# A hybrid decoder layer on one core: an ordering model with a shared port, fewer two-input operations on Pool, and 1/RMS spread by transposes

## The chip, the core and the metric

The kernel runs on 1 core of one Trainium2 chip. The metric is the device time of one execution in microseconds (us). In the profile the engines are PE (TensorE, matrix products; PEld its weight loads), DVE (VectorE), ACT (ScalarE), POOL (GpSimd) and SP (SyncE, which here only starts DMAs). Each engine works through its own queue in order and waits at an instruction until what that instruction needs is there.

## What is computed

One layer of a decoder for a prompt of 1024 tokens and 8 sample sequences of 8 tokens, with shared weights, all in float32. The tokens stand together as 1088 columns.

```python
hn = _rmsnorm(x, lw['norm1_g'])
z = hn @ lw['w_in']                      # q | k | v | u_ssm | u_pool
...                                      # dilated attention, merged over three dilations
...                                      # S5 state space: complex diagonal scan, GELU, GLU
...                                      # trailing mean pooling, linear map
mix = jnp.concatenate([_rmsnorm(att, lw['out_norm_att']),
                       _rmsnorm(ssm_out, lw['out_norm_ssm']),
                       _rmsnorm(pool_out, lw['out_norm_pool'])], axis=-1)
x = x + mix @ lw['w_out']
hn2 = _rmsnorm(x, lw['norm2_g'])
up = hn2 @ lw['w_up']
up_c, conv_state = _causal_dwconv(up, conv_prefix, lw['conv_w'], lw['conv_b'])
a, g = jnp.split(up_c, 2, axis=-1)
x = x + (jax.nn.silu(g) * a) @ lw['w_down']
```

The model width is 1024, the feed-forward width 2816. A last RMSNorm follows, and the new K, V, state, pooling and convolution buffers are outputs too.

## The kernel before

**Products.** Features lie on the 128 partitions, tokens on the free axis. A float32 product is done as three products of operands in two parts: the high part is a cast by ACT, the low part the difference (a two-operand subtraction by DVE or Pool). The split weights of a half tile are called `whl` (three buffers), those of the activations `A`. The input projection, the output projection and the first tiles of the up projection go by `dense_group`: 24 products into one PSUM bank `dps` (two banks), token chunk by token chunk (384, 384 and 320 columns). The rest of the up projection and the down projection are taken in 2 x 2 blocks by seven products (`wino`, Winograd's form), in PSUM banks `wX`, `wY`, `wW`. This needs sums of blocks: of the tokens' features once (`tgen`, tiles X, then `tsplit` into T and A), of the up weights (`uraw`, `wraw`), of the down weights (`draw`, `wraw`, in `dsum` and `dw`) and of the hidden features (`hst`, staged back from memory four tiles at a time, in `hb`), the last two followed by splits into `whl` and `hop`. Each of the 20 steps of the down projection has 14 outputs, which DVE adds to `X` straight from PSUM.

**Beside the products** run, as generators, the parts of the layer that are no large products: the SSM (`ssm_params` and `ssm_tables`: tables of powers, many small operations on Pool; table products `s_pn` on DVE; transposes `rps`; then the scan, the products `yps`, a round trip through memory, GELU, and the products `glu`), prompt attention (scores `S`, transposes `tp`, products `pv`), sample attention, pooling, and the norms. A norm sums squares on PE (`nps`), computes 1/RMS (`rs_x`, `rs_t`, `rs_y`) and spreads it over all partitions on PE (`bcast`, into `nbc`).

**What sets the order.** The program is put down by a planner of its own. `Model.note` (line 87) is called for each instruction before it is issued, from `call` (line 154), and estimates from a table of costs when the instruction will start and end: its engine's queue, when its operands are ready, and a delay between engines. All instructions but DMA starts therefore carry line 156 in the profile, and one goes by the tiles' names. `Driver` steps the generators: each yields the time at which its next step can run, and `tick`, called between products, steps those whose time has come by the model's clock of PE; `until` steps others while a product cannot go on. Which engine makes a two-operand step is chosen by `light(d)` (line 1607): Pool if by the model it would be free `d` us earlier than DVE. `d` is -0.5 for the features' sums and splits, 0 for the down weights' sums, -0.5 and 0.5 for the hidden features' sums and splits, 0.5 for the down weights' splits, 2.5 for the gate, 9 for the up weights. The order on each engine is fixed when the program is built; on the chip only semaphores act.

Of the kernel before, what the change touches and what calls it, by code (L numbers as in the profile page):

```python
# [12 lines left out]
P = 128  # L13
# [22 lines left out]
class Model:  # L36
    """Estimates when each instruction will run; the order in which the independent parts of the kernel
    are put down goes by it."""
    LAT = 0.13
    OWN = {"pe": 0.0, "dve": 0.1}  # L40

    def __init__(self):
        self.free = {}
        self.mem = {}
        self.ring = {}
        self.dma = 0.0
        self.tiled = False

# [9 lines left out]
    def ready(self, *aps, eng=None):  # L58
        """When the last writes to aps are done, as seen by an engine."""
        t = 0.0  # L60
        for ap in aps:
            m, lo, hi = self.seg(ap)
            for b in range(lo, hi + 1):
                if b in m[1]:
                    f, e = m[1][b]
                    t = max(t, f + self.LAT if e != eng else f + self.OWN.get(e, 0.1) if e != "dma" else 0.0)
        return t
# [18 lines left out]

    def note(self, eng, fn, args, kw):
# [14 lines left out]
        else:  # L102
            if eng == "pe":
# [4 lines left out]
                elif args[1].dtype == F32R:  # L108
                    c = 0.0034 + n / 2400.0
                else:  # L110
                    c = 0.005 + max(4 * n / 2400.0, 0.213 * max(np_, 32) / 128.0)
                if np_ < P:
                    # column tiles run beside the first
# [19 lines left out]
            else:  # L133
                c = 0.15 + (2.0e-3 if fn == "tensor_tensor" else 3.35e-3) * n
# [50 lines left out]
class Driver:  # L185
    """Steps the generators of the parts that run beside the large products.  A generator yields when
    its next step can run: a time, a condition, or None for at once."""
# [24 lines left out]
    def pick(self, t):  # L212
        """The generator to step: by priority among those ready at t, else the next to be ready."""
# [26 lines left out]
class Body:  # L240
# [8 lines left out]
    def acq(self, n):  # L249
        """Waits for n PSUM banks of the common ring."""  # L250
# [6 lines left out]
    def act(self, c, q, k):  # L257
        """The high (q = 0) or low part of feature tile k of the activations, token chunk c."""
# [9 lines left out]
    def rsqrt(self, x, n, width, pool=False):  # L268
        """x: [n, width] SBUF, overwritten; gives 1/sqrt(x).  pool: on Pool, else on DVE."""
# [26 lines left out]
    def rstd(self, c, parts, segs, pool=False):  # L296
        """1 / RMS of token chunk c: parts(k0, k1, a) gives the squares to be summed for segment
        (k0, k1, scale), as APs of [128, 128 tokens from a]."""
# [20 lines left out]
    def bcast(self, c, y, bc=None):  # L319
        """y [tokens of a tile, tile] of chunk c as [128, tokens], the same on every partition."""  # L320
# [3 lines left out]
        for ti, (a, w) in enumerate(self.tok_tiles(c)):  # L324
            last = CH[c][1] == 320 and ti == 2
            nc.tensor.matmul(bc[:, a + (64 if last else 0):a + 128], y[:, ti:ti + 1].to_broadcast([P, 128]),
                             self.ident[:, 64:128] if last else self.ident[:, :], start=True, stop=True)
        return bc

# [1 line left out]
    def w_open(self, src, n, alloc=None):  # L331
        """src(i): DRAM AP [128, 4, 128] of half tile i; n: number of halves."""
# [40 lines left out]
    def w_split(self, upto):  # L373
        """Starts the splits of the product's halves before upto."""
# [6 lines left out]
    def dense_group(self, m, c, out_fn, last=True, pool=None):  # L381
        """One (feature tile, token chunk) of a product with K = 1024; last: the tile's last chunk."""
# [5 lines left out]
        for k in range(KD):  # L388
# [11 lines left out]
            if k == 3 and last:  # L400
                if self.w_hold < self.ws["n"]:
                    # the first of the two tiles that share the chunks
# [9 lines left out]
    def prep(self, c, src, gcol):  # L412
        """The activations of chunk c times the gains, in two parts; the RMS is divided out after the
        product."""
# [10 lines left out]
    def put_rms(self, c, y, own=False):  # L425
        """1 / RMS of chunk c to its place, the same on every partition."""
# [10 lines left out]
    # ---------------------------------------------------------------- SSM parameters  # L437
    def pfma(self, out, x, a, y, t):
        """out = x * a + y on Pool (a: immediate)."""
# [4 lines left out]
    def horner(self, p, cs, r):  # L444
        """p = (..((p + c0) * r + c1) * r ..) * r on Pool."""
# [21 lines left out]
    def cmul(self, eng, orr, oi, ar, ai, br, bi, t):  # L467
        """(orr, oi) = (ar + i ai) * (br + i bi); orr, oi differ from the operands; t: scratch."""
# [7 lines left out]
    def ssm_params(self):  # L476
# [48 lines left out]
        # powers of the decay, 0..8  # L525
# [21 lines left out]
        # decay^8 of the modulus, rotation^(8 * 2^k)  # L547
# [10 lines left out]
        # input matrix  # L558
# [20 lines left out]
        # C of both groups of a pair, each with zeros on the other one's states  # L579
# [7 lines left out]
    def ssm_tables(self, hf):  # L587
        """Tables of one half (4 pairs of groups)."""
# [18 lines left out]
        yield None  # L607
        ar, ai = bt(self.pwp[:, 0, q, :]), bt(self.pwp[:, 1, q, :])
        cr, ci = bch(self.bc_in[:, 2, q, :]), bch(self.cneg[:, q, :])
        # the real and the negated imaginary part of C a^n; cneg holds the negated imaginary part of C  # L610
# [11 lines left out]
        # R with (step, channel) on the partitions  # L622
# [10 lines left out]
        # impulse response blocks  # L633
# [38 lines left out]
    def ssm_half(self, hf):  # L672
# [30 lines left out]
        # sample sequences: one chunk each  # L703
# [19 lines left out]
        # rotate back; column c of the chunk buffer holds the state before chunk c  # L723
# [76 lines left out]
    # ---------------------------------------------------------------- pooling mixer  # L800
    def pool_open(self):
        """The scratch is the K and V memory of the next pair."""
# [20 lines left out]
    def pool_in(self, i, c, ps):  # L823
        """Takes chunk c of the pooling input to its buffer, behind the 15 columns before it."""
# [61 lines left out]
    # ---------------------------------------------------------------- prompt attention  # L886
    def att_scores(self, j):
        """Scores of the query blocks and their exponentials; the products with V follow in att_out.
# [1219 lines left out]
def _layout(a):  # L2108
# [6 lines left out]
    out = {}  # L2115
# [94 lines left out]
```

## Time and profile before

| | us |
|---|---|
| time, median of 3 runs (lowest to highest) | 1363.84 (1362.06 to 1365.27) |
| span of the profiled execution | 1362.6 |
| PE busy | 1272.4 |
| DVE busy | 1031.8 |
| POOL busy | 566.7 |
| ACT busy | 539.4 |

The span of the profiled execution, from the first to the last instruction, lies inside the range of the runs' times. By time the stages are: 0 to 80 the norm of the input, the first projections and the SSM's small tables; 80 to 250 input projection beside SSM and prompt attention; 250 to 570 the rest of it, sample attention, the output projection and the second norm; 570 to 640 the first tiles of the up projection and the block sums of its operands; 640 to 1040 the up projection in blocks; 1040 to 1320 the down projection in blocks; then the last pair of tiles and the final norm.

### The profile page before, as it was taken

Reading aid. Unit: us, or ns where it says so; the run is one execution under the profiler, and the core shown is the slowest. Engines: PE = TensorE matmul, PEld = TensorE weight load, DVE = VectorE, ACT = ScalarE, POOL = GpSimd, SP = SyncE. Lnnn points to the kernel's source line nnn. Section 1 sums busy time; section 2 is a strip of 40 time slices with the busy share of each in tenths; the row PEclk is TensorE's granted clock in tenths of the full one; section 3 lists DMA queues with packets and bytes.
Section 4 is the critical chain, followed back from the end, with each engine's and each line's share of the span. In section 5 each row is a group of like instructions: output and inputs, shape, how many; then the busy total and the mean of one; then the engine's idle time right before and its main releaser. Section 6 shows DMA issues by size and latency. Waiting matters only on the chain.

```text
span 1362.6 us, 26926 instructions
## 1 busy us (share of the span) xinstructions
PE 1272.4 (93%) x10466; PEld 1182.9 (87%) x10466; DVE 1031.8 (76%) x1990; ACT 539.4 (40%) x1127; POOL 566.7 (42%) x914
## 2 busy tenths in 40 slices
PE   7699899999999899978999999999999788888997
PEld 7697787777767899977999999999999688888997
DVE  5536765564378932897888888898889989999866
ACT  6222333333245422443545445455454333333333
POOL 7860430210012422593233232332335978768624
PEclk9899999999999999988999999999999889999997
DMA  9221212578874345202231221212212513222213
GB/s 339 87 81 33 68 40 83 183 240 289 281 246 149 83 138 157 65 24 102 106 112 55 88 82 62 95 65 79 95 49 99 186 56 113 97 68 91 81 44 132
DMA packets 80319, 154.84 MB, mean 114 GB/s; under 512 B 9856, under 2 KB 43136, under 8 KB 80192
## 3 DMA queue, kind: packets, MB, share of 16 engines
q1 hardware_dynamic: 78960, 149.68, 33.1%
q10 hardware_dynamic: 1152, 3.04, 0.6%
q8 instruction: 82, 1.34, 0.4%
q14 instruction: 45, 0.37, 0.1%
q0 software_dynamic: 80, 0.41, 0.1%
HBM read 124.04 MB, written 28.47 MB: 112 GB/s over the span
## 4 chain that ended last, share of the span: by engine, by line
PE 68%; DVE 18%; POOL 7%; issue 4%; DMA 1%; ACT 1%; POOLq 0%; DVEq 0%; SPq 0%; ACTq 0%
PE wX L156 23%; PE dps L156 15%; PE wY L156 11%; PE wW L156 5%; DVE X L156 5%; DVE whl L156 3%; POOL ssm_small L156 3%; DVE hop L156 2%; PE pv L156 2%; PE dn L156 2%; PE S L156 2%; DVE P L156 1%; PE yps L156 1%; PE od L156 1%; PE Sp L156 1%
## 5 line engine op out<-in xcount | busy, mean ns | idle before, releaser
L156 PE MATMUL dps<-A,whl 128*128 128x384 f32 (+1 forms) x1896 | 370.3, 344 | 29.7 <-DVE k L156 11.9
L156 PEld LDWEIGHTS dps<-A,whl 128*128 128x128 f32 x1896 | 319.9, 194 | 51.0 <-issue 14.9
L156 PE MATMUL wX<-T,whl 128*128 128x272 f32 x1440 | 193.0, 290 | 4.8 <-DVE whl L156 3.7
L156 PEld LDWEIGHTS wX<-T,whl 128*128 128x128 f32 x1440 | 186.1, 190 | 5.6 <-DVE whl L156 4.1
L156 PE MATMUL wX<-hop,whl 128*128 128x272 f32 x960 | 141.8, 300 | 27.1 <-DVE X L156 21.8
L156 PEld LDWEIGHTS wX<-hop,whl 128*128 128x128 f32 x960 | 130.8, 196 | 32.8 <-issue 12.1
L156 DVE SCALAR_TENSOR_TENSOR cv<-raw,vec,cv 128x1104 f32<-128x1104 f32 x88 | 126.0, 1431 | 12.2 <-ACT cv L156 10.8
L156 POOL TENSOR_TENSOR th<-th,cv 128x64 f32<-128x64 f32 (+1 forms) x40 | 79.8, 2013 | 131.2 <-DVE th L156 127.4
L156 PE MATMUL wY<-A,whl 128*128 128x272 f32 x960 | 127.6, 288 | 0.9 <-DVE whl L156 0.9
L156 PEld LDWEIGHTS wY<-A,whl 128*128 128x128 f32 x960 | 123.3, 188 | 1.1 <-DVE whl L156 1.1
L156 ACT CAST whl<-uraw 128x512 fp32r<-128x512 f32 x120 | 74.8, 623 | 81.0 <-PE wX L156 44.2
L156 ACT CAST whl<-draw 128x256 fp32r<-128x256 f32 (+1 forms) x122 | 47.8, 415 | 143.4 <-POOL draw L156 33.3
L156 POOL COPY cvo<-raw 128x2 f32<-128x2 f32 x88 | 27.6, 343 | 167.2 <-DVE raw L156 154.9
L156 ACT CAST whl<-wraw 128x512 fp32r<-128x512 f32 (+1 forms) x92 | 52.3, 570 | 112.4 <-PE dps L156 63.7
L156 DVE TENSOR_TENSOR whl<-uraw,whl 128x512 fp32r<-128x512 f32 x120 | 87.2, 727 | 12.5 <-ACT whl L156 9.9
L156 DVE TENSOR_TENSOR whl<-wraw,whl 128x512 fp32r<-128x512 f32 (+1 forms) x90 | 67.0, 745 | 31.2 <-ACT whl L156 31.2
L156 DVE TENSOR_TENSOR X<-wX,X 128x272 f32<-128x272 f32 x160 | 66.6, 431 | 14.3 <-PE wX L156 14.0
L156 PE MATMUL wY<-hop,whl 128*128 128x272 f32 x480 | 69.1, 293 | 1.0 <-DVE whl L156 1.0
L156 DVE TENSOR_TENSOR uraw<-uraw 128x512 f32<-128x512 f32 x40 | 69.2, 1729 | 0.7
L156 PEld LDWEIGHTS wY<-hop,whl 128*128 128x128 f32 x480 | 64.6, 193 | 1.6 <-DVE whl L156 1.6
L156 ACT ACTIVATE P<-P,sm 128x128 f32<-128x128 f32 (+7 forms) x64 | 35.7, 558 | 74.0 <-DVE sm L156 74.0
L156 PE MATMUL wW<-A,whl 128*128 128x272 f32 x480 | 63.2, 288 | 0.0
(271 smaller groups left out, 2336.1 us busy)
## 6 DMA issues: line engine op xcount, KB each, us to landing
K<-in_ck_dram SPq DMA_DIRECT2D x40, 512.0 KB, 6.3
V<-in_cv_dram SPq DMA_DIRECT2D x80, 256.0 KB, 4.4
uraw<-in_w_up_dram SPq DMA_DIRECT2D x40, 512.0 KB, 4.0
hs<-th SPq DMA_DIRECT2D x22, 544.0 KB, 2.7
hst<-hs SPq DMA_DIRECT2D x22, 544.0 KB, 5.3
draw<-in_w_down_dram SPq DMA_DIRECT2D x20, 512.0 KB, 3.5
wraw<-in_w_in_dram SPq DMA_DIRECT2D x28, 256.0 KB, 3.1
X<-xs SPq DMA_DIRECT2D x8, 544.0 KB, 4.4
```

The costliest lines, as they stand in the source:

```text
L156: return f(*args, **kw)
```

## The change

**The model's costs.** PE's products of split operands are taken as 0.447 ns for each column (0.417 before), other float32 products a little longer, Pool's two-operand operations as 2.2 ns for each column (2.0 before), and the delay of a result to the same engine as 0.12 us on DVE and Pool (0.1 before).

**The port.** The model now keeps the intervals in which DVE and Pool use a port that they share. Of DVE these are the operations without an operand in PSUM (`two`), of Pool all but memsets. An operation that would start inside an interval of the other engine is taken to start at its end (`clear`).

**Pool's share.** `light(d)` takes Pool only where it would be free more than 2 us before DVE, and never for `d` of 9.

**SSM tables.** The step that makes the products with `ssm_pwp` and `ssm_cneg` on DVE is due when the model has these two ready; before, it was due at once.

**The broadcast of 1/RMS** is three transposes of the column of values, repeated over the columns, in place of three float32 products of it with the identity.

Comments and docstrings are taken out too, which shifts line numbers: line 156 of before is line 174 of after.

```diff
 class Model:
-    OWN = {"pe": 0.0, "dve": 0.1}
+    OWN = {"pe": 0.0, "dve": 0.12, "pool": 0.12}
...
+        self.port = {"dve": [], "pool": []}
+
+    def clear(self, eng, t):
+        other = self.port["pool" if eng == "dve" else "dve"]
+        for a, b in reversed(other[-40:]):
+            if a <= t < b:
+                return self.clear(eng, b)
+        return t
...
+    def two(self, args, kw):
+        x = [a for a in list(args[1:]) + [kw.get("in0"), kw.get("in1")] if hasattr(a, "bitcast") and a.free_size() > 1]
+        return all(a.space != bass.MemoryType.PSUM for a in x)
...
                 elif args[1].dtype == F32R:
-                    c = 0.0034 + n / 2400.0
+                    c = 0.0034 + 0.447e-3 * n
                 else:
-                    c = 0.005 + max(4 * n / 2400.0, 0.213 * max(np_, 32) / 128.0)
+                    c = 0.005 + max(4 * n / 2350.0, 0.218 * max(np_, 32) / 128.0)
...
             else:
-                c = 0.15 + (2.0e-3 if fn == "tensor_tensor" else 3.35e-3) * n
+                c = 0.15 + (2.2e-3 if fn == "tensor_tensor" else 3.35e-3) * n
+            if eng == "pool" and fn != "memset" or eng == "dve" and self.two(args, kw):
+                start = self.clear(eng, start)
+                self.port[eng].append((start, start + c))
...
     def bcast(self, c, y, bc=None):
         for ti, (a, w) in enumerate(self.tok_tiles(c)):
-            last = CH[c][1] == 320 and ti == 2
-            nc.tensor.matmul(bc[:, a + (64 if last else 0):a + 128], y[:, ti:ti + 1].to_broadcast([P, 128]),
-                             self.ident[:, 64:128] if last else self.ident[:, :], start=True, stop=True)
+            nc.tensor.transpose(bc[:, a:a + 128], y[:, ti:ti + 1].to_broadcast([P, 128]), self.ident)
...
     def ssm_tables(self, hf):
         self.cmul(g, rn[:, 0], rn[:, 1], ar, ai, br, bi, t4)
-        yield None
+        yield self.M.ready(self.pwp, self.cneg)
...
     def light(self, d=0.0):
-        return self.nc.gpsimd if self.M.free.get("pool", 0.0) + d < self.M.free.get("dve", 0.0) else self.nc.vector
+        return self.nc.gpsimd if max(d, 2.0) < 9.0 and self.M.free.get("pool", 0.0) + 2.0 < self.M.free.get("dve", 0.0) else self.nc.vector
```

**What moves.** Counted over the whole program, 81 two-operand operations go from Pool to DVE: 48 with 256 columns in the down projection (`draw`, `wraw` and their splits), 18 sums of `hst` and 4 splits `hop` there, ten of the block sums and splits of the up projection's operands (`X`, `T`, `A`), and one of the final norm (`acc`). Besides, a few evictions of PSUM change between DVE and ACT. PE has the same products; the order of the small ones among the dense ones shifts.

The first place is DVE's queue about 50 us in, at the SSM's first tables (`s_pn`, and X_92 as scratch); `k_671` is the K tile that evicts the dense products `dps`. Before:

```order
L156 SCALAR_TENSOR_TENSOR X_85<-dps,rms 128x64
L156 TENSOR_TENSOR s_pn<-ssm_pwp,bc_in 128x512
L156 TENSOR_TENSOR X_92<-ssm_pwp,ssm_cneg 128x512
L156 TENSOR_TENSOR s_pn<-s_pn,X_92 128x512
L156 TENSOR_TENSOR s_pn<-ssm_pwp,ssm_cneg 128x512
L156 TENSOR_TENSOR X_92<-ssm_pwp,bc_in 128x512
L156 TENSOR_TENSOR s_pn<-s_pn,X_92 128x512
L156 TENSOR_TENSOR whl<-wraw,whl 128x512
L156 TENSOR_TENSOR k_671<-dps,rms 128x384 x2
L156 TENSOR_TENSOR whl<-wraw,whl 128x512
L156 TENSOR_TENSOR k_671<-dps,rms 128x320
```

and after:

```order
L174 SCALAR_TENSOR_TENSOR X_85<-dps,rms 128x64
L174 TENSOR_TENSOR whl<-wraw,whl 128x512
L174 TENSOR_TENSOR k_671<-dps,rms 128x384 x2
L174 TENSOR_TENSOR s_pn<-ssm_pwp,bc_in 128x512
L174 TENSOR_TENSOR X_92<-ssm_pwp,ssm_cneg 128x512
L174 TENSOR_TENSOR s_pn<-s_pn,X_92 128x512
L174 TENSOR_TENSOR s_pn<-ssm_pwp,ssm_cneg 128x512
L174 TENSOR_TENSOR X_92<-ssm_pwp,bc_in 128x512
L174 TENSOR_TENSOR s_pn<-s_pn,X_92 128x512
L174 TENSOR_TENSOR whl<-wraw,whl 128x512
L174 TENSOR_TENSOR k_671<-dps,rms 128x320
```

One weight split and the first two evictions of K, which stood behind the six table products, stand ahead of them; the third eviction stays behind. On PE the transposes `rps` that follow come after 39 dense products counted from the end of the second K chunk, and after 42 before.

The second place is PE's queue ahead of the first `glu` of the SSM, about 235 us in. Before, after the last `yps`:

```order
L156 MATMUL vps<-ident,vT 128x128 x3
L156 MATMUL dps<-A_74,whl 128x320 x2
L156 MATMUL dps<-A_82,whl 128x320
L156 MATMUL vps<-ident,vT 128x128 x4
L156 MATMUL pv<-P,v_674 64x128 x4
L156 MATMUL pv<-P,vf_676 64x32 x8
L156 MATMUL S<-k_672,X_86 128x256 x2
L156 MATMUL S<-k_672,X_86 32x192 x8
L156 MATMUL dps<-A_75,whl 128x320 x2
L156 MATMUL dps<-A_83,whl 128x320
L156 MATMUL glu<-X_91,s_t 128x408
L156 MATMUL glu<-X_92,s_t 128x408
```

and after (the last dense product ahead of `glu` stands eight rows ahead of the first one shown):

```order
L174 MATMUL tp<-ident,P 32x128
L174 MATMUL tp<-ident,P 128x128 x2
L174 MATMUL S<-k_672,X_86 128x256 x2
L174 MATMUL S<-k_672,X_86 32x192 x8
L174 MATMUL pv<-P,v_674 64x128 x4
L174 MATMUL pv<-P,vf_676 64x32 x16
L174 MATMUL tp<-ident,P 128x128
L174 MATMUL tp<-ident,P 64x128
L174 MATMUL tp<-ident,P 128x128 x3
L174 MATMUL tp<-ident,P 64x128
L174 MATMUL tp<-ident,P 128x128 x2
L174 MATMUL glu<-X_91,s_t 128x408
```

The dense products between the last `yps` and the first `glu` fall from 54 to 21, and what stands right before `glu` is attention alone. The last `yps` come 36 dense products later than before, and the second half's transposes `rps` 24 later.

The third place is Pool's queue in the down projection, where the second group of hidden features comes in (`hst` their sums, `hop` their split, `draw` and `whl` the weights' sums and splits). Before:

```order
L156 TENSOR_TENSOR draw<-draw 128x256
L156 TENSOR_TENSOR whl<-draw,whl 128x256 x3
L156 TENSOR_TENSOR draw<-wraw,draw 128x256
L156 TENSOR_TENSOR hop<-hst,hop 128x544
L156 TENSOR_TENSOR hst<-hst 128x544 x5
L156 TENSOR_TENSOR whl<-draw,whl 128x256
L156 TENSOR_TENSOR hst<-hst 128x544
L156 TENSOR_TENSOR draw<-wraw,draw 128x256
L156 TENSOR_TENSOR hop<-hst,hop 128x544 x2
```

and after:

```order
L174 TENSOR_TENSOR whl<-draw,whl 128x256 x2
L174 TENSOR_TENSOR hop<-hst,hop 128x544
L174 TENSOR_TENSOR hst<-hst 128x544 x3
L174 TENSOR_TENSOR whl<-draw,whl 128x256
L174 TENSOR_TENSOR hst<-hst 128x544
L174 TENSOR_TENSOR hop<-hst,hop 128x544 x2
L174 TENSOR_TENSOR whl<-draw,whl 128x256
L174 TENSOR_TENSOR hst<-hst 128x544
L174 TENSOR_TENSOR hop<-hst,hop 128x544
```

The sums of `hst` came five in a row and one more; now three, one and one, with fewer of the weights' operations between. The rest of these sums stand on DVE.

## Rows read from the trace of the kernel before

**Rows 1.** The page's first part: busy us (share of the span), instructions.

```profile
PE 1272.4 (93%) x10466; PEld 1182.9 (87%) x10466; DVE 1031.8 (76%) x1990; ACT 539.4 (40%) x1127; POOL 566.7 (42%) x914
```

**Rows 2.** Busy us by stage (start:end, length), then PEclk, DMA share, GB/s.

```profile
0.00:80.00 80.00, 60.16 (x338) 58.70 (x338) 41.21 (x102) 32.01 (x59) 61.63 (x222) 0.91 0.58 199
80.00:250.00 170.00, 163.95 (x1476) 136.86 (x1476) 105.07 (x262) 53.35 (x132) 42.84 (x112) 0.97 0.20 56
250.00:570.00 320.00, 310.59 (x3124) 258.99 (x3123) 190.40 (x556) 108.19 (x254) 71.58 (x135) 1.00 0.59 191
570.00:640.00 70.00, 55.36 (x314) 53.59 (x313) 63.23 (x66) 31.42 (x60) 47.65 (x51) 0.89 0.18 60
640.00:1040.00 400.00, 400.00 (x3185) 400.00 (x3185) 350.01 (x473) 196.66 (x362) 118.81 (x188) 1.00 0.24 82
1040.00:1290.00 250.00, 219.38 (x1595) 212.17 (x1594) 233.91 (x411) 93.18 (x210) 197.57 (x178) 0.95 0.29 99
1290.00:1362.00 72.00, 62.91 (x446) 62.57 (x444) 47.95 (x125) 24.61 (x52) 26.61 (x31) 0.90 0.25 89
```

**Rows 3.** What PE waited for: us in total, times, longest.

```profile
PE wX L156 <- DVE X L156: 21.8, 15, 4.0
...
PE dps L156 <- DVE whl L156: 11.3, 4, 7.1
```

**Rows 4.** Timeline, 1102 to 1112: start, us, engine, operation [idle before <-releaser].

```profile
1102.32 8.07 POOL L156 TENSOR_TENSOR hst<-hst 128x544 f32<-128x544 f32 x5
...
1102.93 3.33 DVE L156 TENSOR_TENSOR hop<-hst,hop 128x544 fp32r<-128x544 f32 x2
...
1106.53 2.67 DVE L156 TENSOR_TENSOR whl<-draw,whl 128x256 fp32r<-128x256 f32 x2
...
1110.04 2.38 PE L156 MATMUL wX<-hop,whl 128*128 128x272 f32 x9 [4.03 <-DVE X L156]
...
1110.85 0.41 DVE L156 TENSOR_TENSOR whl<-draw,whl 128x256 fp32r<-128x256 f32 x1
```

**Rows 5.** Groups by form, 1040 to 1160: count, busy us, mean ns, idle before.

```profile
L156 DVE TENSOR_TENSOR hst<-hst 128x544 f32<-128x544 f32 x1 | 0.7, 707 | 0.0
...
L156 POOL TENSOR_TENSOR whl<-draw,whl 128x256 fp32r<-128x256 f32 x22 | 19.1, 875 | 10.7 <-ACT whl L156 10.7
```

**Rows 6.** Timeline, 36 to 80: the stop at the SSM tables.

```profile
47.42 9.57 PE L156 MATMUL dps<-A,whl 128*128 128x320 f32 x54
...
62.85 0.55 POOL L156 TENSOR_SCALAR ssm_cneg<-bc_in 128x128 f32<-128x128 f32 x1
...
63.43 0.69 DVE L156 TENSOR_TENSOR X<-ssm_pwp,ssm_cneg 128x512 f32<-128x512 f32 x1 [12.50 <-POOL ssm_cneg L156]
...
66.88 1.54 DVE L156 TENSOR_TENSOR whl<-wraw,whl 128x512 fp32r<-128x512 f32 x1
...
68.94 9.60 PE L156 MATMUL dps<-A,whl 128*128 128x320 f32 x42 [11.95 <-DVE k L156]
...
72.80 1.28 POOL L156 TENSOR_TENSOR X<-X,X 128x512 f32<-128x512 f32 x1
```

**Rows 7.** Chain that ended last: start, us, what; one broadcast, one row of transposes.

```profile
78.54 0.87 PE rps L156 x8
...
258.63 0.79 PE nbc L156 x6
```

**Rows 8.** Timeline, 160 to 240: the second half of the SSM.

```profile
162.26 1.09 PE L156 MATMUL tp<-ident,P 128*128 128x128 f32 x8 [2.01 <-DVE P L156]
...
212.44 0.73 PE L156 MATMUL yps<-X,s_pn 64*128 64x136 f32 x4
...
231.46 1.28 DVE L156 SCALAR_TENSOR_TENSOR X<-s_rm,s_tmp 128x1088 f32<-128x1088 f32 x1
```

## The prediction

> **What bounds the kernel now.** I read the page's first part, then a table of the busy time by stage, then the list of what TensorE (PE) waited for, and then the timeline at the places that list points to. [rows 1] say that PE is the engine to look at: 1272.4 us busy of 1362.6, so at most 90 us can come from its idle time. [rows 2] say where. From 640 to 1040 PE is busy for all 400 us at the full clock: whatever else moves there, nothing can be gained. From 80 to 570 it is idle for 15 us of 490. The idle time sits in three places: 20 us before 80, 15 us from 570 to 640, 31 us from 1040 to 1290, and the granted clock falls below 1 in the same stages (0.91, 0.89, 0.95; the clock has two levels, 1.2 and 2.4 GHz, so a mean of 0.95 is a tenth of the stretch at the lower one). [rows 3] name the releaser in the last two: VectorE (DVE), by its additions into X and by its part of the weight splits. So the stages outside 640 to 1040 hang on DVE, which is 94% busy from 1040 to 1290, and the question is what the change does to DVE's queue there.
>
> **How long things take alone and beside Pool.** [rows 4] show the burst that costs most. Pool runs five sums of hst in 8.07 us, 1.61 each. In that time DVE needs 3.33 us for two operations of the size that takes 0.71 alone ([rows 5]), and 2.67 us for two of the size that takes 0.41 alone. So DVE lost 3.33 - 1.42 = 1.9 and 2.67 - 0.82 = 1.85 us, together 3.8 us beside 8.07 us of Pool, 0.47 us for each us; the additions into X stood behind it, and PE stood still for 4.03 us.
>
> **Down projection (1040 to 1290): fewer operations on Pool.** By the counts of the program 48 operations of 256 columns and 22 of 544 leave Pool for DVE here. DVE gets 48 x 0.41 + 22 x 0.71 = 35.3 us. Pool loses 48 x 0.875 ([rows 5]) + 22 x 1.61 = 77.4 of 197.6 us. At the burst's rate that gives DVE back 0.47 x 77.4 = 36.4 us, so DVE's total hardly moves (-1 us). What does change is the shape of the queue: the five sums in a row become three, one and one, and an addition into X waits behind operations of 0.4 and 0.7 us rather than behind 3.3 us. I take 3 of the 31 idle us for that. The bounds: if nothing came back, DVE would have 35 us more where it has 250 - 233.9 = 16 free, and the stage would be 19 us longer; if Pool's time all came back, the idle 31 us could go. I take a value near zero because the burst's rate, the row nearest to it, gives zero.
>
> **570 to 640: the same edit.** Ten operations, nine of 544 columns, leave Pool for DVE: about 10 x 0.71 = 7.1 us more, 0.47 x 16.1 = 7.6 us less. The weight splits that PE waits for here (11.3 us over the run, [rows 3]) stand about as far back as before, one of them behind seven sums in place of two. I take -1, from -6 to +5.
>
> **The new wait in the SSM tables.** [rows 6] show the largest single stop of PE: DVE stands at its second table product until Pool has written ssm_cneg (63.43, idle 12.50 before it), three evictions of k are queued behind it, and PE, out of PSUM banks at 57.0, is idle for 11.95 us. The change puts one weight split and two of these evictions ahead of the table products. It does not follow that 12 us are gained. PE then does the third part of k (24 products; 54 took 9.57 us, so 4.3 us, to 61.2) and half of the first part of v (12 products, 2.1 us, to 63.3). The other half of v's weights is split behind the six table products, which still begin at 63.43 and took until 66.9, and the split until 68.4. And 39 products after the stop (42 before the change) PE comes to the transposes rps, which need Pool's last table sum, done at 72.80 + 1.28 = 74.08. Before they started at 78.54; now not before 74.1. That is at most 4.4 us, and as PE is idle before them for nearly as long as before (two stops of 5 us), some of it goes to the lower clock. I take -2.5, from -4.5 to 0. What hides the rest is Pool's own chain of small operations, which the change does not touch.
>
> **1/RMS by transposes.** A broadcast of one chunk is six matrix passes of 0.79 us now; eight transposes of the same size take 0.87, so three take 0.33 ([rows 7]). That is 0.46 us less, 18 times. The first three lie before 74.1, where Pool sets the end: nothing. Nine for the mixer and three for the second norm lie where PE is 97% busy (250 to 570, [rows 2]): 12 x 0.46 = 5.5, of which I take 5.0, since the last three also wait for DVE. Of the final three the last is on the path to the end: 0.5. Together -5.5, from -2 to -8.
> On this the Trainium skill speaks against the change (TensorE: Matmul & The Clock Gate, Part 4: PE-mode transpose): it says that the full clock does not engage for a transpose as it does for a matmul. By that a broadcast would run at the lower level, 0.66 us rather than 0.33, and the twelve in the middle would gain 1.6 us rather than 5.5. Here the trace does not bear it out: by the program's order 250 to 570 holds some 180 of the 272 transposes of attention scores, at a granted clock of 1.00 ([rows 2]).
>
> **80 to 250: other order, same work.** The numbers of the planner also move SSM work against the dense products. The second half's transposes come 24 products later, which spares PE waits like the 2.01 us of [rows 8] (3.6 us in all there, with the clock at 0.97 over 170 us, 5 us). But its last yps come 36 products later, while glu must still follow the same chain: 212.4 for the last yps, 232.7 (231.46 + 1.28) for its last step on DVE ([rows 8]), 20 us. Between the two PE now has 21 dense products where it had 54, and attention, about 15 us by the durations before. So about 5 us of new idle time against 4 to 8 saved. I take 0, from -8 to +6.
>
> **The sum.** -3 - 1 - 2.5 - 5.5 + 0 = -12. The profiled execution's span, 1362.6, lies inside the runs' times, so the sum is set against the median: 1363.8 - 12 = 1352 us.
>
> **The rivals.**
> *DVE's jams dissolve.* If half of PE's 21.8 us behind the additions ([rows 3]) went, and half of what the clock costs in that stage (0.05 x 250 = 12.5), 17 us rather than 3 would be gained there: 1338. For it: DVE has idle time between the jams. Against it: DVE is 94% busy. Chance 0.12.
> *Given back.* Pool's table chain and the clock leave nothing of the first stop, glu costs 4 us, and the down projection 2 more: 1363.8 - 5.5 - 1 + 6 = 1363. This is also what one would see if the new numbers of the planner are no nearer to the chip than the old ones. Chance 0.13.
> *DVE overfull, the slower side.* With fewer Pool operations left, each meets a DVE that is more often at an operation with two SBUF operands, so what comes back for each us taken from Pool may be less than 0.47. At 0.2 DVE gets 35.3 - 15.5 = 20 us more in a stage in which it is 94% busy; the stage grows by as much, and the rest gives 9: 1375. It decides below about 0.30, where 35.3 - 0.30 x 77.4 = 12 us eat the other gains. For it: the two-operand work of DVE grows by half. Against it: the one jam that the timeline shows in full. Chance 0.16.
> *Transposes cool the clock.* Two stretches more at the lower level, 5 us each as the one from 80 to 250, where little but transposes runs, and most of the gain is gone: 1362. Against it: the clock of 1.00 from 250 to 570. Chance 0.03. This is what the rule of the Trainium skill above (TensorE: Matmul & The Clock Gate, Part 4: PE-mode transpose) would come to.
>
> **How the numbers follow.** The forecast has 0.56, its own range is 1341 to 1360. A measurement of this kernel can tell about 0.2% from no change, 2.7 us: faster is below 1361.1, slower above 1366.6. Faster: 0.56 + 0.12 = 0.68. Same: 0.13 + 0.03 = 0.16. Slower: 0.16. The range reaches from 1336, which holds nearly all of the first rival, to 1367, which holds the second and leaves out the slower one: about 0.18 outside.
>
> **What would show it.** Right: the stop before rps shorter by about 4 us and still ended by Pool; the broadcasts at 0.33 us; DVE's busy time from 1040 to 1290 within 10 us of 234 while Pool's falls from 198 to about 120; PE's waits for DVE's additions somewhat under 21.8; 640 to 1040 unchanged. Wrong: rps starting well before 74 us, DVE's busy time falling in the down projection (much more comes back than 0.47) or PE's waits for it growing (less does), or a new stop of more than 6 us ahead of glu.

## The result, and the profile after

The changed kernel takes 1376.9 us (median of 4 runs, 1373.84 to 1383.38) against 1364.55 for the kernel before, a ratio of 1.0108 with a 95% interval of 1.0085 to 1.0131: slower, where faster was forecast. The profiled execution has a span of 1372.0 us, the low end of its runs, 9.4 us over the profile of before.

The page's first part after the change answers [rows 1]; the second line is the span with the mean granted clock, which was 0.970 before.

```profile
PE 1278.6 (93%) x10412; PEld 1184.1 (86%) x10412; DVE 1041.2 (76%) x2071; ACT 538.3 (39%) x1129; POOL 466.5 (34%) x831
```
```profile
core 0: 1372.0 us, clock 0.962
```

Pool gave up 100 us, DVE took on 9. PE's idle time went from 1362.6 - 1272.4 = 90.2 to 1372.0 - 1278.6 = 93.4 us, by 3.2 only. Its busy time rose by 6.2 us, although 54 passes fewer are made. The clock explains that: (1 - clock) x span is the time at full speed that was not granted, (1 - 0.970) x 1362.6 = 40.9 us before and (1 - 0.962) x 1372.0 = 52.1 after, 11 us more (a part of it in idle time, where it costs nothing). I call it the missing clock below.

To see where, the next views cut both executions at the same places of the program: the end of `glu`, the end of the pooling map, the first block product, the first down product, the first of the last pair of tiles. Columns as in [rows 2]; before first, then after.

```profile
0.00:249.80 249.80, 223.91 (x1811) 195.36 (x1812) 146.28 (x363) 85.22 (x190) 104.48 (x334) 0.95 0.32 102
249.80:464.90 215.10, 209.75 (x2505) 159.70 (x2505) 138.92 (x445) 77.73 (x191) 36.52 (x84) 1.00 0.70 229
464.90:634.40 169.50, 153.71 (x922) 150.60 (x920) 109.12 (x170) 60.73 (x121) 80.93 (x97) 0.96 0.28 87
...
1058.00:1315.80 257.80, 229.72 (x1683) 223.16 (x1682) 234.82 (x433) 93.07 (x211) 192.25 (x179) 0.95 0.27 94
```
```profile
0.00:249.30 249.30, 222.24 (x1802) 192.88 (x1803) 150.56 (x372) 81.78 (x181) 101.78 (x334) 0.96 0.32 102
249.30:467.00 217.70, 205.44 (x2457) 153.78 (x2456) 137.88 (x431) 79.92 (x201) 37.59 (x84) 0.98 0.70 228
467.00:639.00 172.00, 161.39 (x934) 157.93 (x933) 104.19 (x183) 60.56 (x122) 64.67 (x89) 0.94 0.26 83
639.00:1062.30 423.30, 419.07 (x3313) 418.43 (x3314) 371.21 (x504) 205.45 (x380) 126.59 (x196) 0.99 0.26 86
1062.30:1323.00 260.70, 232.48 (x1682) 224.13 (x1682) 246.76 (x499) 93.43 (x210) 122.59 (x114) 0.94 0.27 95
1323.00:1372.00 49.00, 37.97 (x233) 36.91 (x231) 30.58 (x86) 17.18 (x36) 13.31 (x14) 0.82 0.25 92
```

The loss is spread: +2.6 us from `glu` to the pooling map, +2.5 to the first block product, +2.9 in the down projection, +2.2 in the tail; the up projection keeps its time. Each of these differences is below the 4 us by which two profiles of one and the same order can differ in a stage (last section), so they say that the loss does not sit in one place, and not how it is shared out. What PE waited for after the change (us in total, times, longest) answers [rows 3]:

```profile
PE dps L174 <- DVE whl L174: 18.3, 5, 7.5
PE wX L174 <- DVE X L174: 11.7, 14, 2.3
...
PE tp L174 <- DVE P L174: 5.9, 6, 3.8
PE rps L174 <- POOL X L174: 3.8, 2, 2.2
PE dps L174 <- DVE vT L174: 3.6, 1, 3.6
```

The waits for DVE's additions into X fell from 21.8 to 11.7 us, as was hoped. But in the down projection alone PE's idle time is 28 us before (257.8 - 229.7) and after (260.7 - 232.5): waits for `hop` and for ACT's part of the splits came in their place. And outside it there are new stops. One is the first `whl` row's longest, in the timeline at 452 to 463 (columns as in [rows 4]):

```profile
456.73 1.94 DVE L174 TENSOR_TENSOR v<-v 128x452 f32<-128x452 f32 x3
...
458.70 2.60 DVE L174 SCALAR_TENSOR_TENSOR X<-v,k 64x256 f32<-64x256 f32 x4
...
461.81 1.28 DVE L174 TENSOR_TENSOR whl<-wraw,whl 128x512 fp32r<-128x512 f32 x2
...
462.55 1.01 PE L174 MATMUL dps<-A,whl 128*128 128x384 f32 x2 [7.54 <-DVE whl L174]
```

DVE works through the pooling sums (`v`, and X from `v` and `k`) before it comes to a weight split that PE has stood waiting for since 455. The planner put them in this order; before, nothing stops PE there for more than 1.4 us, and the same two splits stand ahead of these sums, in the timeline of before at 455 to 463:

```profile
457.96 1.28 DVE L156 TENSOR_TENSOR whl<-wraw,whl 128x512 fp32r<-128x512 f32 x2
...
459.82 1.94 DVE L156 TENSOR_TENSOR v<-v 128x452 f32<-128x452 f32 x3
```

With the stop the granted clock falls from 1.00 to 0.50, its lower level, and stays there for 13.7 us (after, columns as in [rows 2]):

```profile
436.00:455.00 19.00, 16.73 (x138) 14.96 (x135) 17.23 (x38) 6.85 (x17) 8.92 (x12) 1.00 0.23 74
...
460.00:473.70 13.70, 11.15 (x37) 10.27 (x38) 10.27 (x37) 3.63 (x8) 3.11 (x3) 0.50 0.20 59
```

Two more stops are new: 3.61 us at 155.7 (an eviction, `vT`) and 3.76 at 233.0, ahead of `glu`.

The SSM stop of [rows 6] after the change, from the timeline at 52 to 80, Pool first and then PE:

```profile
62.64 0.55 POOL L174 TENSOR_SCALAR ssm_cneg<-bc_in 128x128 f32<-128x128 f32 x1
```
```profile
68.27 1.01 PE L174 MATMUL dps<-A,whl 128*128 128x384 f32 x2 [5.19 <-DVE whl L174]
70.85 1.12 PE L174 MATMUL rps<-ident,X 128*128 128x128 f32 x4 [1.58 <-POOL X L174]
74.22 1.12 PE L174 MATMUL rps<-ident,X 128*128 128x128 f32 x4 [2.25 <-POOL X L174]
```

11.95 us have become 5.19 + 1.58 + 2.25 = 9.0, and the second half of `rps` starts at 74.22, on Pool's last sum, 4.3 us earlier than before; the first four, which needed an earlier sum, start at 70.85. At the end of `glu` only 0.5 us of it is left (249.8 to 249.3).

### The profile page after: what moved, and what is told of

Its sections match the earlier page's. It is cut to its first block, busy times and chain, and to the rows that moved or that the text cites. A ratio compares the mean times of both kernels' runs of the same rounds, so it can differ in the third digit from the quotient of the medians.

```text
span 1372.0 us, 26762 instructions
## 1 busy us (share of the span) xinstructions
PE 1278.6 (93%) x10412; PEld 1184.1 (86%) x10412; DVE 1041.2 (76%) x2071; ACT 538.3 (39%) x1129; POOL 466.5 (34%) x831
## 4 chain that ended last, share of the span: by engine, by line
PE 70%; DVE 18%; POOL 6%; issue 3%; DMA 1%; ACT 1%; SPq 0%; POOLq 0%; DVEq 0%; ACTq 0%
PE wX L174 22%; PE dps L174 16%; PE wY L174 11%; PE wW L174 5%; DVE X L174 5%; POOL ssm_small L174 3%; DVE hop L174 3%; DVE whl L174 2%; PE pv L174 2%; PE S L174 2%; PE od L174 2%; PE Sp L174 1%; PE tp L174 1%; PE yps L174 1%; DVE P L174 1%
## 5 line engine op out<-in xcount | busy, mean ns | idle before, releaser
L174 PE MATMUL wX<-hop,whl 128*128 128x272 f32 x960 | 144.0, 302 | 24.4 <-DVE X L174 11.7
L174 DVE SCALAR_TENSOR_TENSOR cv<-raw,vec,cv 128x1104 f32<-128x1104 f32 x88 | 122.5, 1393 | 12.1 <-ACT cv L174 10.8
L174 ACT CAST whl<-uraw 128x512 fp32r<-128x512 f32 x120 | 74.8, 624 | 82.7 <-PE wX L174 44.2
```

What stands on the lines that cost most here:

```text
L174: return f(*args, **kw)
```

## The experiments

The four parts are called model (costs and port), share (`light`), wait (`ssm_tables`) and broadcasts. Where a run makes or undoes one of them whole, its diff is that part of the diff above, and is not repeated. Theory F: DVE is overfull because of the share. Theory O: the planner's new numbers set an order with new stops of PE. Theory C came up after the first runs: which stops an order meets is an accident of the numbers, so that any small change of them moves the time. Gains in us are differences of medians to the kernel before in the same round (its medians lie between 1363.8 and 1365.0); the ratios come with a 95% interval.

### Each part alone, on the kernel before

e1, broadcasts, with the planner still booking the old products, so that no engine's order moves:

```diff
+            self.M.note("pe", "matmul", (bc[...], y[...], ident), {})
+            nc.tensor.real.transpose(bc[:, a:a + 128], y[:, ti:ti + 1].to_broadcast([P, 128]), self.ident)
-            nc.tensor.matmul(bc[...], y[...], ident, start=True, stop=True)
```

> The kernel before with the 18 broadcasts of 1/RMS done by transposes; the planner still books them as the old matrix products, so every engine keeps its order. By the prediction's term (0.46 us each, most of them on PE's path): -5.5, about 1359 us, stretches at the low clock as before. By the trace of after, where PE's work at full speed is 3.9 us less: -3 to -4, about 1361. By the rival in which transposes cool the clock: 1362 to 1367, with new low stretches beside the broadcasts (258 to 278, 415 to 483).

Measured: 1360.0 us, ratio 0.9959 (0.9934 to 0.9984), -4.2 us. The row of the tile `nbc` (least, median and most ns, first and last start; before, then e1) shows that each of the 54 passes takes what each of the old 108 took, so they ran at the same clock:

```profile
L156 PE MATMUL nbc<-ident,rs_y x108: 222/275/582, 25.8 to 1354.9; 128*128 128x128 f32 x96, 128*128 128x64 f32 x12
L328 PE MATMUL nbc<-ident,rs_y x54: 271/273/473, 27.1 to 1346.7; 128*128 128x128 f32 x54
```

The stretches beside the broadcasts, 258 to 278 and 415 to 483, have a granted clock of 1.00 in e1. By that the rule of the Trainium skill weighed in the prediction (TensorE: Matmul & The Clock Gate, Part 4: PE-mode transpose) does not show here.

e2, wait:

```diff
-        yield None
+        yield self.M.ready(self.pwp, self.cneg)
```

> The kernel before with only the new due time in the SSM tables. Prediction's term: -2.5 (-4.5 to 0), the start of rps at 74 to 76 in place of 78.4, nothing given back later. If the new stop ahead of glu at 233 us in the trace of after (3.8 us idle and 6.8 us at the low clock) comes from this edit: 0 at the end of glu, total within 2 us of before. If it comes from the planner's numbers: the gain of the first stop stays (idle and clock, 8 to 10 us by the trace of after at rps), about 1355.

Measured: 1360.6, ratio 0.9954 (0.9936 to 0.9972). `rps` start at 74.8, and there is no stop ahead of `glu`. A stop of 3.75 us that ends at 148.8 is new, but `glu` ends at 242.8 (249.8 in the profile of before, 245.6 in that of e3 with the same order): nothing is given back.

e3, share: the new `light` alone.

> The kernel before with only the new rule for Pool's share (64 two-operand operations of the down projection go to DVE). Theory F (DVE overfull): it carries most of the loss, 1369 to 1376, with the growth between 1040 and 1325. Theory O (order: the planner's new numbers make new stops of PE before 640): 1362 to 1367, the down projection within 3 us of before's 257.7. Prediction: about 1360.

Measured: 1359.9, ratio 0.9969 (0.9949 to 0.9989). The down projection takes 257.4 us, before 257.8. Theory F falls: the share alone costs nothing. Where it gains was not found: by its profile e3 is 3.6 us ahead already at 584 us, where the first instruction that it moves stands, and so with before's order, and 5.8 at the first block product.

e4, model: the numbers of `OWN` and `note`, and the port.

> The kernel before with only the planner's new numbers and the port in its model; the old rule for Pool's share, the old wait, the old broadcasts. Theory O: slower, 1370 to 1380, with a stop of several us behind DVE's weight splits between 430 and 480 and one ahead of glu, each followed by a stretch at the low clock. Theory F: within 3 us of before, 1361 to 1367.

Measured: 1367.0, ratio 1.0016 (0.9999 to 1.0033). Its first block product stands at 638.9 (634.4 before), with other stops than after's. A little slower at most, and not clear of noise; Theory O gets only a part of what it wants.

### All but one part

e5 to e8 are the changed kernel with one part put back: the model, the share, the wait, the broadcasts.

> After without the planner's new numbers and port: broadcasts, wait and share together on the old model. If the three gains of the single runs (-4.2, -3.7, -4.2) add: 1352, the forecast's own time. Theory O (the planner's numbers set an order that makes new stops): near 1352, no stop over 5 us from 430 to 480, none ahead of glu. Theory F (more operations on DVE, worst together with the rest): over 1366. Theory C (any new order may land well or badly, by chance of where the stops fall): anywhere from 1352 to 1375, its stops at places that no part explains.

> After with the old rule for Pool's share. Theory F: the loss goes, 1358 to 1364, and the stages before 570 stay as in after. Theory O: the stops at 233 and 455 us stay, since no share is decided there; 1371 to 1377, within 5 us of after (1376.9). Theory C: stages before 570 as in after, down projection within 4 us either way.

> After with the old due time in the SSM tables. Theory O: the stop at 455 stays and the first stop is back at about 12 us; 1376 to 1382. If the new numbers and the wait together make the stops at 233 and 455: these two go (about 20 us idle and low clock by the trace of after), the first stop is back, 1364 to 1368.

> After with the old broadcasts (which the planner books at three times the time, so its order moves too). If the transposes only do their own work: 4 us slower than after, about 1381. If the new stop at 455 comes from the order that their shorter times give: it goes, and the time is 1365 to 1370. Theory C: a change of either sign that the broadcasts' own time does not explain.

Measured: e5 1354.4 (0.9936, 0.9913 to 0.9959), e6 1375.3 (1.0091, 1.0065 to 1.0116), e7 1369.3 (1.0035, 1.0015 to 1.0054), e8 1379.4 (1.0116, 1.0086 to 1.0147). So wait, share and broadcasts together gain 9.7 us on the old model, which lies in the forecast's range, and beat both kernels. The model takes back 22.5 us. The share is not guilty: without it the time stays. The stops at 155.7, 233 and 455 are in e6 and e8, and in neither e4 nor e7: it takes the new numbers together with the wait to make them (and, as e15 shows below, not just any new numbers). The kernels that have the first two (after, e6, e8, e9, e13) end `glu` at 249 to 256 us, e2, e5 and e16, with the wait on the old model, at 243 to 244. Without the wait they are gone, but the first stop is back with 13.3 us (e7).

### Taking the stop away

e9: the two splits behind the stop at 455 go to Pool, which is idle there; booked as before, so that nothing else moves.

```diff
-        self.nc.vector.tensor_tensor(hl[:, 1], r, hl[:, 0].bitcast(F32), ALU.subtract)
+        e = Engine(self.nc.gpsimd.real, "dve", self.M) if i in (34, 35) else self.nc.vector
+        e.tensor_tensor(hl[:, 1], r, hl[:, 0].bitcast(F32), ALU.subtract)
```

> After, with the two weight splits (34 and 35) that end the stop at 455 us made by Pool, which is idle there, in place of DVE; the planner books them as before, so all else keeps its order. Theory O (the stop is the split's place behind pooling work in DVE's queue): the stop falls from 7.5 us to 0 to 2, the low stretch after it (13.7 us, half of it lost) gets shorter by 3 to 14: 1364 to 1371 against after's 1376.9. If another thing is late behind it (its activations, a DMA of weights): a stop of 5 us or more stays there, 1374 to 1379.

Measured: 1374.9, ratio 1.0088 (1.0055 to 1.0121). The wait for the split is down to 0.80 us, but a sum of squares stands behind the splits on Pool now, as the timeline of e9 shows (columns as in [rows 4]):

```profile
461.63 0.62 PE L174 MATMUL dps<-A,whl 128*128 128x384 f32 x2 [0.80 <-POOL whl L174]
...
465.42 1.37 POOL L174 TENSOR_TENSOR sq_p<-sq_p 128x384 f32<-128x384 f32 x1
...
466.84 1.44 PE L174 MATMUL nps<-ones,sq_p 128*128 128x1 f32 x6 [4.59 <-POOL sq_p L174]
```

e13 gives that sum to DVE as well:

```diff
+                    if (k0, c) == (6, 1):
+                        e = Engine(nc.vector.real, "pool", self.M)
+                    e.tensor_tensor(acc, acc, t, ALU.add)
```

> After, with the two weight splits on Pool as in e9, and the sum of squares of the pooling norm, which was late behind them, on DVE; the planner books all as before. If the loss lies in the stops of this order: the two stops from 455 to 475 (6.6 us in e9, 7.5 in after) fall to 0 to 3, and the time to 1366 to 1371. If the loss lies elsewhere in the order (first 250 us, down projection): 1373 to 1377.

Measured: 1378.4, ratio 1.0084 (1.0057 to 1.0111). The stop is back whole, in front of the norm, in the timeline of e13:

```profile
467.27 3.58 DVE L174 TENSOR_TENSOR v<-v 128x452 f32<-128x452 f32 x3
470.88 1.13 DVE L174 SCALAR_TENSOR_TENSOR X<-v,k 64x256 f32<-64x256 f32 x4
...
472.91 0.55 DVE L174 TENSOR_TENSOR sq_p<-sq_p 128x384 f32<-128x384 f32 x1
...
473.52 1.44 PE L174 MATMUL nps<-ones,sq_p 128*128 128x1 f32 x6 [7.68 <-DVE sq_p L174]
```

So the split was only the first of several that waited for the same backlog of pooling work: PE's queue has the pooling norm there whatever is split where. The edit also cost DVE time: the three `v` sums, 1.94 us in after, take 3.58 beside Pool's splits. It missed its aim, and it cannot say what the stop costs.

### One number changed

e10 and e11 take out one half of the model, the port or the costs, from the changed kernel; e12 and e15 change a product's cost in it from 0.447 ns for each column to 0.430 and 0.460; e14 and e17 change that cost in the kernel before, where it is 0.417, to 0.430 and 0.405; e18 does so in e5. e16 is e5 without the share.

```diff
-                    c = 0.0034 + 0.447e-3 * n
+                    c = 0.0034 + 0.43e-3 * n
```

> After without the port in the model, the new costs kept. If the port's delays set the order with the four stops (156, 233, 455, 481 us in after): they go, 1354 to 1362. If the costs do it: they stay, 1372 to 1380. Theory C (which stops an order meets is an accident of the numbers): they go or move to other places, and the time lies between.

> After with the old costs (products, Pool's operations, delay to the same engine), the port kept. If the costs do it: 1354 to 1362, the four stops gone. If the port does it: 1372 to 1380. Theory C: the four stops gone here as well as without the port.

> After with one number changed by 4%: a product's cost 0.430 ns for each column in place of 0.447. Theory C: the stops at 156, 233 and 455 go or move by this alone, and the time changes by more than 5 us, 1355 to 1370. If it is the mechanism of the model (port, wait) and not the place where its numbers happen to lie: same stops, 1374 to 1380.

> The kernel before with one number changed: a product's cost 0.430 ns for each column in place of 0.417 (3%). Theory C (any small change of the planner's numbers moves the time by several us, either way, since it moves the stops): more than 3 us from before, 1352 to 1361 or 1367 to 1377. If only the port together with the new costs is harmful: within 3 us of 1364.

> After with a product's cost 0.460 ns for each column in place of 0.447 (3% the other way). Theory C: other stops, 1355 to 1372. If larger product costs are what harms (0.417 in e5: 1354, 0.430 in e12: 1360, 0.447: 1377): 1377 to 1390.

> The kernel before with the wait and the broadcasts, without the share. If the single gains add (-4.2, -3.7): 1356, and the share's own gain is 2 us or less beside them. If the share brings 4 us here too: 1358 to 1360. If it harms: 1350 to 1353.

> The kernel before with a product's cost 0.405 ns for each column in place of 0.417 (3% the other way than e14). Theory C: more than 3 us from before, of either sign, 1352 to 1361 or 1367 to 1377. If a larger product cost is what harms: 1355 to 1364.

> The three edits of e5 on the old model, with a product's cost of 0.430 in place of 0.417. If the three edits' gain is their own whatever the order: 10 us under before with 0.430 (e14, 1377.0), so 1367. If 1354.4 belongs to the edits and any other order costs the same as before's with 0.430: 1375 to 1380. Theory C in full: anywhere from 1352 to 1378.

| kernel | product's cost | median us | ratio to before (95%) | PE idle us | clock |
|---|---|---|---|---|---|
| e17: before | 0.405 | 1359.0 | 0.9965 (0.9950 to 0.9979) | 90.9 | 0.973 |
| before | 0.417 | 1364.6 | 1 | 90.2 | 0.970 |
| e14: before | 0.430 | 1377.0 | 1.0080 (1.0063 to 1.0097) | 95.0 | 0.964 |
| e16: wait, broadcasts | 0.417 | 1360.3 | 0.9964 (0.9946 to 0.9981) | 93.4 | 0.976 |
| e5: and share | 0.417 | 1354.4 | 0.9936 (0.9913 to 0.9959) | 90.2 | 0.971 |
| e18: as e5 | 0.430 | 1372.1 | 1.0062 (1.0034 to 1.0090) | 96.0 | 0.961 |
| e11: after, old costs | 0.417 | 1357.3 | 0.9953 (0.9926 to 0.9979) | 90.6 | 0.974 |
| e12: after | 0.430 | 1360.2 | 0.9966 (0.9946 to 0.9987) | 90.7 | 0.967 |
| after | 0.447 | 1376.9 | 1.0108 (1.0085 to 1.0131) | 93.4 | 0.962 |
| e15: after | 0.460 | 1359.5 | 0.9955 (0.9936 to 0.9973) | 86.6 | 0.967 |
| e10: after, no port | 0.447 | 1364.6 | 1.0008 (0.9993 to 1.0023) | 92.2 | 0.968 |

Idle time and clock are those of one profiled execution; that of e5 took 1361.0, 6.6 us over its median.

Theory C holds as far as the times go. With 3% more or 4% less for one cost, the changed kernel is 17 us faster; with 3% more, the kernel before is 12 us slower. There is no direction in it: 0.430 is the slow number on the old model and a quick one on the new. Nor does one stop decide: e10 has after's stop at 455 whole, and is 12 us faster; from its timeline:

```profile
460.34 1.01 PE L174 MATMUL dps<-A,whl 128*128 128x384 f32 x2 [7.55 <-DVE whl L174]
```

Of after's three stops e12 keeps the one at 156 (3.29 us) and e15 none. And e14, as slow as after, has no stop of 2.5 us or more from 140 to 490, like e11, which is 20 us faster. So that the time moves is shown; that it moves by way of these stops is not.

e16 against e5: the share is worth 4 us by the ratios and 6 by the medians beside the other two edits on the old model, at the edge of the noise. e18 against e14: the three edits together are worth 5 us by the medians on the order with 0.430, 2.5 by the ratios, whose intervals overlap, and 10 on the one with 0.417.

## Why the prediction was wrong, point by point

**What was right.** The three edits that it costed with care: their sum was -12 and measures -9.7 (e5), by the ratio's interval -5.6 to -11.9. That it comes so near is in part luck: of the runs with these edits only e1 keeps before's order, and with the product's cost at 0.430 the three are worth only half as much or less (e18 against e14). The signs it named came for the most part: Pool's last sum ends the SSM stop, with the second half of `rps` at 74.22 (74.1 was worked out); the broadcasts are three passes of the old length; the waits for additions fell from 21.8 to 11.7; 639 to 1062 kept its time; from 1040 to 1290 DVE's busy time is 242.9 us (within 10 of 234), Pool's 125.9. One sign of being wrong came too: the first four of `rps` start well before 74, at 70.85, since not all eight need the last sum. All these signs watch the edits, and they were right in a kernel that is 12 us slower.

**Broadcasts**, -5.5: e1 -4.2, by the ratio's interval -2.2 to -9.0, so the term held within the noise. 0.33 us for three passes was too short: in the timeline the broadcast at 258 us takes 0.51 after and 0.94 before. The difference, 0.43, is near the 0.46 that I took.

**Wait**, -2.5: e2 -3.7, nothing given back on the old model. With the new numbers `glu` ends 6 to 13 us later than in e2, with the stops at 155.7 and 233 us: the one ahead of `glu`, for which I had put about 5 us of idle time, is there with 3.76.

**Share**, -3 and -1: e3 -4.4 in all, but not from where I said. The stage of the down projection stayed (257.4). Between the cuts of after 48 operations of 256 columns and 20 of 544 came to DVE, 33.9 us by my prices, and two of `th` left it, 2.3 us. DVE was busy 11.9 us longer (234.8 to 246.8), so 33.9 - 2.3 - 11.9 = 19.7 us came back for 192.3 - 122.6 = 69.7 us of Pool: 0.28, not the 0.47 of one burst [rows 4], which was not the mean. The 12 us more fitted into DVE's idle time, 257.8 - 234.8 = 23 us before.

**The step that failed** is the one that costed the planner's numbers: "other order, same work", 0 from -8 to +6, and for 80 to 250 us only. Their whole effect is +22.5 us beside the other edits (e5 to after), and +2.8 alone. I had costed one neighbourhood where I had seen rows move, and took the rest of the order as kept. The bound was too small even as a bound: one number 3 or 4% off moves either kernel by 5 to 17 us, and this could not be read from any row of before. What could be read was that the change touches numbers on which each later choice hangs, so that no term for its sign could be worked out; a term of 0 with more than 20 us on either side would have been honest. And one of the new places could have been seen: the order of after was known, and the two weight splits stand behind the pooling sums in it and ahead of them before. From 250 to 570 us I had looked at no queue.

**The rivals.** DVE overfull gave 1375, which is near the measured time, for a wrong reason: with the old rule (e6) it is 1375.3 too, and its stage grew by 2.9 us and not 20. Its condition came true (0.28 is below the 0.30 at which it was to decide), but the work went into idle time of DVE. "Given back" came nearest as a mechanism (it names new numbers no better than the old), at 14 us too little. The cooling by transposes is refuted by e1 (faster, and no new low stretch beside the broadcasts).

**What stays open** is why one order costs 10 or 20 us more than another with the same work. The profiles say in which form. The eight kernels whose profile is longer than 1367 us (after, e6 to e9, e13, e14, e18) have a mean span of 1374.4, 95.9 us of idle PE and a clock that misses 51.9 us; the other twelve 1359.0, 90.2 and 38.5. So of 15.4 us of span, 5.7 are idle time and 9.7 a longer busy time of PE, with 13.4 us more of missing clock; the work is the same but for the broadcasts. Idle time does not tell the rest: e16 and after make the same number of passes (10412) and are idle for 93.4 us each, but PE is busy for 1263.6 us in the one and 1278.6 in the other, at a clock of 0.976 and 0.962. Which stops an order has differs from one to the next, and after's were not settled: the two runs that went for one of them did not get rid of it.

## What to carry to other kernels

When a change touches the numbers of a greedy planner, cost the edits if you like, but give the order itself a term of its own with a range taken from trials: build the kernel before with one number a few per cent off, both ways, and see how far the time goes. A model meant to be truer need not give a faster kernel, and one timing of it says little on whether the model is better; judge an edit with the order held fixed (book the old instruction, issue the new one), or over several numbers. And keep in the final kernel the number that measured best.

## What the runs showed of the hardware

The same order does not lose the same to the clock each time. Up to 250 us e3 has before's order instruction for instruction, and e1 all but the broadcasts; from 150 to 180 us the granted clock was 0.83 in before's profile (first row) and 0.94 in e3's (second), with PE busy for 26.4 us in both and 18 products more done in e3 (columns as in [rows 2]):

```profile
150.00:180.00 30.00, 26.43 (x206) 25.25 (x204) 17.79 (x29) 8.43 (x18) 21.05 (x49) 0.83 0.23 57
```
```profile
150.00:180.00 30.00, 26.45 (x224) 24.43 (x223) 18.04 (x33) 9.25 (x22) 20.76 (x50) 0.94 0.29 83
```

The end of `glu` came at 249.8 in the one and 245.6 in the other, 4 us apart, of the 10 us by which the runs of one kernel differ (before: 1360.1 to 1369.9). A difference of 4 us between two profiles in one stage is therefore no finding here; between the medians it is one.

And idle time is not all that an order costs: by the means of eight and twelve kernels above, 5.7 us more of idle PE came with 13.4 us more of missing clock and 9.7 us more of busy PE. A sum that counts idle time alone, as mine did in most of its terms, counts less than half of that difference.
